# Feed-forward gate and up products of a decoder layer: from pairs of tiles with the weights stationary to four pairs of tiles with the tokens stationary

## The chip, the cores and the metric

The kernel runs on one core of one Trainium2 chip. The metric is the device time of one execution in microseconds (us). The kernel before took 1340.99 us, the median of three runs (1340.22 to 1342.37). One further execution was recorded by the hardware profiler; its own time is 1339.9 us, its span from the first to the last instruction 1338.1 us.

## What is computed

One layer of a decoder on 512 tokens of width 1024: a feed-forward half-step, a token mixing of three branches, and a second feed-forward half-step, each between two RMS norms. All is float32. The change concerns the two feed-forward steps alone:

```python
def swiglu(x, w_gu, w_down):          # x: 512 x 1024
    g, u = jnp.split(x @ w_gu, 2, axis=-1)   # w_gu: 1024 x 5632
    return (jax.nn.silu(g) * u) @ w_down     # w_down: 2816 x 1024

h = h + 0.5 * rmsnorm(swiglu(rmsnorm(h, pre_w), w_gu, w_down), post_w)
```

The width 2816 is 22 tiles of 128 columns, in the gate as in the up half of `w_gu`.

## The kernel before, in words

**Precision.** Every float32 operand of a matmul is split into a high part (ScalarE writes it, rounded: `split`, L173) and a low part (VectorE writes the rest: L168). A product is then three matmuls: high by high, high by low, low by high.

**Seven products for eight.** The gate and up columns of the same index are computed together. The token matrix is cut into quarters (256 tokens by 512 of the 1024 input columns), and so is the pair of weight tiles (512 input rows by the gate or the up tile). Winograd's form of Strassen's scheme gets the four quarters of the result from seven quarter products, numbered 1 to 7, at the price of sums and differences of quarters. The token sums t1 to t4 are made once per feed-forward step (`combine`, L244). The weight sums s1 to s4 are made for each pair (`wops`, L313): one or two of them by a DMA that accumulates (L334), the others by VectorE. The results are put together from PSUM (`pair`, L411, and `gu`, L600).

**Form of a product.** In `product` (L393) the weights are the stationary operand (128 x 128) and the tokens move, 256 columns at a time, so that the result has the gate or up columns on the partitions and the tokens along the free axis. This is the form in which the down projection needs it as its stationary operand. One pair of tiles takes 7 x 4 x 3 = 84 matmuls of 256 columns.

**Order.** The first two gate and two up tiles (the heads) are done without the scheme. The other twenty pairs follow one by one. The 22 tiles are grouped into chunks (`CHUNKS1` and `CHUNKS2`, L44), and while a chunk's pairs are computed, the down products of the chunk before it are mixed in (L680): one call of `down` is one token tile and one half of the output columns, 12 matmuls of 512 columns for a chunk of four. Their sums go to `y` in SBUF. The down products of the last chunk (six tiles in the first step, four in the second) come at the end, with the norm behind them. Except for the opening and the last two token tiles, the engine order is set by the compiler's scheduler, which follows the order of the code and the clock that the code advances by `tick`.

**Buffers.** Weight pieces arrive in `st` (4 buffers), `sum` (5) and `st2` (2); split weights lie in `w` (18), everything else in 37 slots of 128 x 512 (`s`). PSUM has 5 banks `ps` and 3 banks `px`. SyncE (SP) issues nearly all loads, in one queue and in order; GpSimd (POOL) issues the accumulating DMAs.

## Time and profile before

| | before |
|---|---|
| median of three runs | 1340.99 us |
| profiled execution, its own time | 1339.9 us |
| its span | 1338.1 us |
| TensorE (PE) busy | 1325.7 us, 99% |
| VectorE (DVE) busy | 1043.0 us, 78% |
| ScalarE (ACT) busy | 753.9 us, 56% |
| DMA, mean over the span | 137 GB/s |
| granted TensorE clock | 0.999 of full speed |

In this profile a matmul's duration reaches over the start of the next one, since matmuls are pipelined. What one matmul costs is read from the distance between two starts, not from its duration. The same holds for VectorE to a lesser degree.

### The profile page before, as it was taken

To read this page: it belongs to the slowest core of one execution; us is meant where nothing else is said; L and a number is where in the kernel's file an instruction comes from. 1 tells how busy PE (TensorE), PEld (TensorE's weight loads), DVE (VectorE), ACT (ScalarE), POOL (GpSimd) and SP (SyncE) were. 2 spreads that over 40 slices of the span, in tenths; PEclk is the share of its full clock that TensorE was granted. 3 is DMA by queue.
4 is the path that set the end of the run, shared out by engine and by line. 5 is a ranking of instruction groups with operands and counts; after the bars stand their busy time and mean duration, and the time that the engine had idled before them with its cause. 6 is when DMAs were issued, how large, how long until landed. Compare 5 with 4: busy or idle time off the path is not lost.

```text
span 1338.1 us, 24335 instructions
## 1 busy us (share of the span) xinstructions
PE 1325.7 (99%) x9228; PEld 1234.3 (92%) x9228; DVE 1043.0 (78%) x1979; ACT 753.9 (56%) x1557; POOL 87.3 (7%) x116
## 2 busy tenths in 40 slices
PE   9999999999999999999999999999999999999997
PEld 8999999999898988899899999999899999999996
DVE  7987777687897975699769968888488877777765
ACT  7764544465566764455765755566366644445541
POOL 1011110110100000000000000000011111111100
PEclk9999999999999999999999999999999999999999
DMA  9587556565425335434223423334536766556523
GB/s 252 153 191 172 144 147 165 126 160 191 161 65 157 111 98 175 122 106 125 65 79 112 119 80 95 103 106 150 193 111 161 187 162 153 143 142 154 146 64 126
DMA packets 238611, 183.14 MB, mean 137 GB/s; under 512 B 11129, under 2 KB 200990, under 8 KB 238494
## 3 DMA queue, kind: packets, MB, share of 16 engines
q1 hardware_dynamic: 223702, 159.49, 39.6%
q0 software_dynamic: 10368, 18.88, 8.6%
q10 hardware_dynamic: 4424, 3.22, 0.8%
q8 instruction: 72, 1.18, 0.4%
q14 instruction: 45, 0.37, 0.1%
HBM read 153.21 MB, written 9.47 MB: 122 GB/s over the span
## 4 chain that ended last, share of the span: by engine, by line
PE 64%; DVE 2%; DMA 1%; ACT 0%; issue 0%; POOLq 0%; DVEq 0%; ACTq 0%
PE ps L381 16%; PE ps L399 12%; PE ps L400 12%; PE ps L401 12%; PE px L381 7%; PE px L386 4%; PE px L390 1%; DVE w L168 1%; DMA st<-in_ffn_w_gu_dram 0%; DVE s L168 0%; DMA sh<-in_w_in_dram 0%; DMA st<-in_w_out_dram 0%; DVE s L736 0%; ACT w L173 0%; DVE st L996 0%
## 5 line engine op out<-in xcount | busy, mean ns | idle before, releaser
L173 ACT ACTIVATE w<-sum 128x512 fp32r<-128x512 f32 x288 | 180.3, 631 | 210.4 <-PE ps L400 183.4
L168 DVE TENSOR_TENSOR w<-sum,w 128x512 fp32r<-128x512 f32 x288 | 196.8, 687 | 72.8 <-ACT w L173 71.8
L399 PE MATMUL ps<-xhi,w 128*128 128x256 f32 x864 | 244.7, 283 | 0.1
L400 PE MATMUL ps<-xlo,w 128*128 128x256 f32 x864 | 244.5, 283 | 0.0
L401 PE MATMUL ps<-xhi,w 128*128 128x256 f32 x864 | 244.5, 283 | 0.0
L173 ACT ACTIVATE w<-st 128x512 fp32r<-128x512 f32 x240 | 150.1, 630 | 116.2 <-PE ps L400 84.0
L168 DVE TENSOR_TENSOR w<-st,w 128x512 fp32r<-128x512 f32 x248 | 168.5, 687 | 32.1 <-ACT w L173 29.4
L381 PE MATMUL px<-s,s 128*128 128x512 f32 x816 | 193.0, 390 | 0.0
L168 DVE TENSOR_TENSOR s<-s,s 128x256 f32<-128x256 f32 (+3 forms) x317 | 176.4, 562 | 14.9 <-ACT s L173 3.9
L381 PEld LDWEIGHTS px<-s,s 128*128 128x128 f32 x816 | 150.6, 188 | 29.9 <-DVE s L168 0.4
L399 PEld LDWEIGHTS ps<-xhi,w 128*128 128x128 f32 x864 | 165.5, 192 | 2.5 <-ACT s L408 0.5
L400 PEld LDWEIGHTS ps<-xlo,w 128*128 128x128 f32 x864 | 165.5, 192 | 2.0
L401 PEld LDWEIGHTS ps<-xhi,w 128*128 128x128 f32 x864 | 165.5, 192 | 0.0
L168 DVE TENSOR_TENSOR sum<-sum,st 128x512 f32<-128x512 f32 x176 | 120.3, 685 | 7.1 <-issue 3.9
L168 DVE TENSOR_TENSOR s<-s,ps 128x256 f32<-128x256 f32 (+1 forms) x195 | 93.0, 477 | 29.2 <-PE ps L381 22.1
L399 PE MATMUL ps<-t3hi,w 128*128 128x256 f32 x288 | 83.6, 290 | 0.0
L168 DVE TENSOR_TENSOR s<-s,px 128x512 f32<-128x512 f32 x73 | 49.8, 683 | 43.0 <-PE px L381 34.8
L399 PE MATMUL ps<-t4hi,w 128*128 128x256 f32 x288 | 82.1, 285 | 0.0
L399 PE MATMUL ps<-t1hi,w 128*128 128x256 f32 x288 | 82.0, 285 | 0.0
L401 PE MATMUL ps<-t2hi,w 128*128 128x256 f32 x288 | 81.7, 284 | 0.0
L401 PE MATMUL ps<-t3hi,w 128*128 128x256 f32 x288 | 81.7, 284 | 0.0
L399 PE MATMUL ps<-t2hi,w 128*128 128x256 f32 x288 | 81.6, 283 | 0.0
(198 smaller groups left out, 2996.6 us busy)
## 6 DMA issues: line engine op xcount, KB each, us to landing
st<-in_ffn_w_gu_dram SPq DMA_DIRECT2D x48, 512.0 KB, 5.0
st<-in_w_in_dram SPq DMA_DIRECT2D x48, 512.0 KB, 3.8
st<-in_ffn_w_down_dram SPq DMA_DIRECT2D x44, 512.0 KB, 4.0
sum<-in_ffn_w_gu_dram SPq DMA_DIRECT2D x80, 256.0 KB, 3.4
sh<-in_ffn_w_gu_dram SPq DMA_DIRECT2D x40, 256.0 KB, 3.3
sum<-st POOLq DMA_DIRECT2D x40, 256.0 KB, 3.3
sum<-sh POOLq DMA_DIRECT2D x32, 256.0 KB, 3.6
sum<-in_w_in_dram SPq DMA_DIRECT2D x32, 256.0 KB, 2.9
```

The lines of the kernel that those rows point to most:

```text
L168: ins = self.nc.vector.tensor_tensor(out=out, in0=a, in1=b, op=op)
L173: self.pin(self.nc.scalar.activation(hi, src, AF.Copy))
L381: self.pin_pe(mm(out, lhsT=lhs[l], rhs=rhs[r], start=a, stop=b))
L386: self.nc.tensor.matmul(out, lhsT=lhsT, rhs=rhs, start=start, stop=stop, **k)
L390: self.pin_pe(self.nc.tensor.transpose(out, in_, self.ident))
L399: mm(out, lhsT=lh, rhs=rh, start=first and k == 0, stop=False, skip_group_check=True)
L400: mm(out, lhsT=lh, rhs=rl, start=False, stop=False, skip_group_check=True)
L401: mm(out, lhsT=ll, rhs=rh, start=False, stop=k == 3, skip_group_check=True)
```

## The change

The twenty pairs of a feed-forward step become five groups of four pairs (`wide`, one per group): four gate tiles side by side are one block of 512 columns, four up tiles another.

- **Product.** In `wide_product` the tokens are stationary (128 tokens by 128 input columns) and 512 weight columns move. A product of a group is 2 token tiles x 4 x 3 = 24 matmuls of 512 columns into two banks, a group 168.
- **Weights.** Pieces are 128 rows by 512 columns. Operands 5 and 7 of a group are formed by DMA (a load and an accumulating load, both from HBM); in each step's first group operand 5 is formed by VectorE. Operands 6 and 3 are VectorE additions into the buffers of operands 1 and 2.
- **Turning the result.** The result now has tokens on the partitions. For each group and token tile the product of silu(gate) and up is transposed on VectorE in blocks of 32 x 32 (`Turn`), stored to DRAM, read back in another order (both on SP's queue), and split into high and low parts. That makes 4 block transpositions, 4 stores and 4 loads back per group, 40 of each in the kernel.
- **Down products.** A unit is now one tile and one half of the output columns for all four token tiles: 12 matmuls into four banks. `DOWNS` says how many units stand behind which product of a group. Of the last group's input in the first step one tile (`TAIL`) is left to the final part, which so has five tiles instead of six.
- **Order.** From the second group on, `strict` holds every engine to the order of the code, which is written out by hand. Background tasks are advanced only outside of these groups. One such task (loading and preparing small parameters of the token mixing) so runs at the end of the first step.

The core of the diff, without the unchanged helpers:

```diff
-CHUNKS1 = (2, 4, 4, 4, 2, 6)
-CHUNKS2 = (2, 4, 4, 4, 4, 4)
+DOWNS = ((0, 1, 0, 1, 0, 1, 1), (0, 0, 2, 2, 2, 1, 1), (0, 0, 2, 2, 1, 0, 0), (0, 0, 1, 1, 1, 0, 0), (0, 0, 1, 0, 1, 0, 0))
...
+EARLY, TAIL = 2, 1
...
+        def add(n):
+            if n == 6:
+                for k, x in enumerate(rest):
+                    self.tt(raw[5][k], raw[5][k], x, ALU.add)
+            raw[n] = raw[{6: 1, 3: 2}[n]]
+            for k in range(4):
+                self.tt(raw[n][k], raw[n][k], raw[{6: 5, 3: 6}[n]][k], ALU.add)
+
+        def cut(j):
+            return [self.wsplit(raw[j][k]) for k in range(4)]
...
+    def wide_product(self, banks, w, j, first=True):
+
+        x = self.xop[j]
+        for t in range(2):
+            ts = slice(t * P, (t + 1) * P)
+            for k in range(4):
+                lh, ll = x[0][:, k, ts], x[1][:, k, ts]
+                for n, (l, r) in enumerate(((lh, w[k][0]), (lh, w[k][1]), (ll, w[k][0]))):
+                    self.pin(self.nc.tensor.matmul(banks[t], lhsT=l, rhs=r, start=first and k == n == 0, stop=k == 3 and n == 2, skip_group_check=True))
+                self.tick(3 * 0.2268)
...
-                        gu(begun or next(pairs), act[-1])
-                        begun = None
-                if before:
-                    for i in range(8 * j // n, 8 * (j + 1) // n):
-                        down(i % NT, i // NT, before[2], ws, before[0] == 0)
...
+        class Turn:
...
+                ins = nc.vector.transpose(blocks.rearrange("p (b f i) -> p f b i", b=4, f=4), g.rearrange("p (f j b) -> p f b j", f=4, b=4))
...
+                self.pin(nc.sync.dma_start(out=d.mem.rearrange("a j b x -> (a j) (b x)"), in_=d.blocks))
...
+                ins = nc.sync.dma_start(out=d.x.rearrange("p (a x) -> p a x", a=4), in_=d.mem.rearrange("a j b x -> (j b) a x"))
...
+            self.wide_product(p, w[s, 4], 4, False)
+            d.make(d.done + 2)
+            d.evict()
+            for i in range(2):
+                self.tt(v[i], v[i], u[i], ALU.subtract)
...
+            cut(s + 1, 1)
+            q = two()
+            for i in range(2):
+                self.tt(q[i], p[i], u[i], ALU.subtract)
+                self.tt(g[i], g[i], q[i], ALU.mult)
+                turns[i] = Turn(g[i])
+                turns[i].store()
...
+                wides[s + 1][1](6)
+            d.run(plan[5])
+
+            self.wide_product(c, w[s, 3], 3, False)
+            d.make(d.done + (3 if end else 2))
+            d.run(plan[6])
+            g = two()
+            for i in range(2):
+                turns[i].back()
+            for i in range(2):
+                self.tt(g[i], u[i], c[i], ALU.add)
+                self.copy(g[i], g[i], AF.Silu)
+                self.tt(g[i], g[i], v[i], ALU.mult)
+                turns[2 + i] = Turn(g[i])
+                turns[2 + i].store()
...
+            def early_rest(turns=turns):
+                for i in range(2, 4):
+                    turns[i].back()
+
+            def late_rest(hl=hl, turns=turns):
+                for i in range(NT):
+                    hl[i] = hl[i] or turns[i].act()
+            late = early_rest, d.evict, late_rest
```

`late` is called in the next group: the loads back of the last two token tiles behind its first product, the addition of the old down sums to `y` and the splitting of the turned tiles behind its second. A group's products stand in the order 1, 2, 6, 5, 7, 4, 3.

How the instructions move is shown at three places. In each the instruction's line comes first, then its operation, what it writes and what it reads (for a matmul the moving operand first, the stationary one second).

TensorE, first feed-forward step, the end of a pair's last product and the down products behind it. Before, `t4` is the token operand of product 4, `w` a weight, `px` the bank of a down product, and `s` the weights and activations of the down product:

```order
L399 MATMUL ps391_1933<-t4hi_98,w399_1999 128x256
L400 MATMUL ps391_1933<-t4lo_99,w399_1999 128x256
L401 MATMUL ps391_1933<-t4hi_98,w400_2000 128x256
L381 MATMUL px403_2025<-s331_1666,s118_603 128x512
L381 MATMUL px403_2025<-s332_1667,s118_603 128x512
L381 MATMUL px403_2025<-s331_1666,s119_604 128x512
```

In the change, the end of a group's product 3 (`xhi1`, `xlo1` are the tokens) and the unit of down products behind it:

```order
L650 MATMUL ps464_1924<-w507_2089,xhi1_89 128x512
L650 MATMUL ps464_1924<-w508_2090,xhi1_89 128x512
L650 MATMUL ps464_1924<-w507_2089,xlo1_91 128x512
L780 MATMUL px511_2097<-s517_2153,s431_1811 128x512
L780 MATMUL px511_2097<-s518_2154,s431_1811 128x512
L780 MATMUL px511_2097<-s517_2153,s432_1812 128x512
```

The gate and up matmuls have changed places of their operands and are twice as wide; the down matmuls keep their form.

VectorE, first step. Before, the evictions of one pair's results amid weight splits (`w`) of the next:

```order
L168 TENSOR_TENSOR s443_2212<-s425_2104,ps431_2127 128x256
L168 TENSOR_TENSOR w498_2462<-st449_2252,w497_2461 128x512
L168 TENSOR_TENSOR s444_2213<-ps434_2145,s425_2104 128x256
L168 TENSOR_TENSOR s443_2212<-s443_2212,s444_2213 128x512
L168 TENSOR_TENSOR w504_2485<-sum502_2481,w503_2484 128x512
L168 TENSOR_TENSOR s416_2074<-s443_2212,s415_2073 128x512
```

In the change, the end of a group: the last block transposition (L817) of the first half of the tokens, the four additions for the next group's operand 6, the gate, product and transposition of the second half of the tokens (banks `ps463` and `ps464` are those of product 3), and the first split of the next group's operand 2:

```order
L817 STREAM_TRANSPOSE s531_2185<-s440_1828 128x4x4x32
L168 TENSOR_TENSOR st490_2003<-st490_2003,sum451_1873 128x512
L168 TENSOR_TENSOR st490_2003<-st490_2003,sum452_1876 128x512
L168 TENSOR_TENSOR st491_2005<-st491_2005,sum453_1879 128x512
L168 TENSOR_TENSOR st491_2005<-st491_2005,sum454_1882 128x512
L168 TENSOR_TENSOR s533_2241<-s401_1695,ps463_1923 128x512
L168 TENSOR_TENSOR s533_2241<-s533_2241,s494_2033 128x512
L817 STREAM_TRANSPOSE s537_2250<-s533_2241 128x4x4x32
L168 TENSOR_TENSOR s534_2242<-s402_1696,ps464_1924 128x512
L168 TENSOR_TENSOR s534_2242<-s534_2242,s495_2034 128x512
L817 STREAM_TRANSPOSE s539_2257<-s534_2242 128x4x4x32
L168 TENSOR_TENSOR w546_2290<-st509_2093,w545_2289 128x512
```

The evictions are 512 wide instead of 256, the transpositions are new, and all of the second half's chain now stands ahead of the next group's weight splits. ScalarE's silu stands between the addition and the product of each token tile.

SP's queue, first step. Before, loads of weights alone (`st`, `sum` and `sh` are buffers of gate, up and down weights):

```order
L155 DMA st553_2801<-in_ffn1_w_down_dram 128x2x512
L155 DMA st558_2811<-in_ffn1_w_down_dram 128x2x512
L155 DMA sum567_2827<-in_ffn1_w_gu_dram 128x4x128
L155 DMA sum568_2830<-in_ffn1_w_gu_dram 128x4x128
L155 DMA st565_2823<-in_ffn1_w_gu_dram 128x8x128
L155 DMA sh566_2825<-in_ffn1_w_gu_dram 128x4x128
```

In the change, at the end of a group (`turn` is the DRAM scratch):

```order
L145 DMA st509_2093<-in_ffn1_w_gu_dram 128x2x512
L145 DMA st510_2095<-in_ffn1_w_gu_dram 128x2x512
L825 DMA turn530_2181<-s529_2179 128x512
L825 DMA turn532_2187<-s531_2185 128x512
L830 DMA s535_2243<-turn530_2181 128x4x128
L830 DMA s536_2245<-turn532_2187 128x4x128
L825 DMA turn538_2252<-s537_2250 128x512
L825 DMA turn540_2259<-s539_2257 128x512
L830 DMA s553_2305<-turn538_2252 128x4x128
L830 DMA s554_2307<-turn540_2259 128x4x128
L145 DMA s555_2309<-in_ffn1_w_down_dram 128x512
L145 DMA s556_2311<-in_ffn1_w_down_dram 128x512
```

Four stores and four loads back now stand in the queue between the last gate and up load of a group and the down weights of the next, and each waits for what it moves.

More of the change, by code (lines that the diff above doesn't have):

```diff
@@ L114, in tick @@
         self.t += us
-        while not self.polling:
+        while not self.polling and self.opening == self.strict:
             due = [x for x in self.tasks if x[0] <= self.t]
@@ L288, in wsplit @@
         hi, lo = self.unit(src.shape, slot), self.unit(src.shape, slot)
-        self.split(hi, lo, src)
+        with ExitStack() as wait:
+            for ins in () if self.strict else self.opened:
+                wait.enter_context(self.tc.issue_after(ins))
+            self.split(hi, lo, src)
         return hi, lo
@@ L588, in ffn @@
+    def ffn(self, w_gu, w_down, w_post, ready, reload, after, early, last=False):
         nc = self.nc
@@ L625, in new_act, with down, cut, fetch @@
             return self.slot(dt=F32R), self.slot(dt=F32R)
-        def down_weights(f, hf):
-            st = self.load(w_down, f, 2, hf * 512, 512)
-            return [self.wsplit(st[:, j, :], slot=True) for j in range(2)]
-        def down(t, hf, act, ws, first, bank=self.paux, cs=slice(0, 512)):
-            acc = bank((P, cs.stop - cs.start))
-            self.proj_N(acc, act, slice(t * P, (t + 1) * P), [(w[0][:, cs], w[1][:, cs]) for w in ws])
-            if first:
-                nc.scalar.copy(y[t][hf], acc)
-            else:
-                self.tt(y[t][hf][:, cs], y[t][hf][:, cs], acc, ALU.add)
+        def down(t, hf, cs):
+            acc = self.psum((P, cs.stop - cs.start))
+            lhs = act(t)
+            for k in [*range(2, n), 0, 1]:
+                self.mm3(acc, lhs[k], [x[:, cs] for x in ws[k, hf]], k == 2, k == 1)
+            self.tt(y[t][hf][:, cs], y[t][hf][:, cs], acc, ALU.add)
+        tail = 0 if last else TAIL
+        wides = [self.wide(w_gu, f * P, DFF + f * P, f == early) for f in range(early, NF, 4)]
+        w = {}
+        def cut(s, j):
+            if s < len(wides):
+                w[s, j] = wides[s][2](j)
+        def fetch(s, j):
+            if s < len(wides):
+                wides[s][0](j)
         tasks, heads = [], []
@@ L686, in ffn @@
[L686 to L696 removed]
+        fetch(0, 1), fetch(0, 2), fetch(0, 5)
@@ new lines, in ffn, with begin @@
+        bank = lambda: [self.psum() for _ in range(2)]
+        two = lambda: [self.slot() for _ in range(2)]
+        def begin(s):
+            a, u = bank(), two()
+            self.wide_product(a, w[s, 1], 1)
+            return a, u
+        if resumed:
+            self.need(*tasks[0])
+            for wg, ac in heads:
+                gu_plain(wg, ac, slice(0, HT))
+            cut(0, 1)
+            begun = begin(0)
+            self.need(*tasks[1])
+        for wg, ac in heads:
+            gu_plain(wg, ac, slice(HT, T))
@@ new lines, in ffn, with final_load, final_cut @@
+        ws, spare = {}, list(self.spare())
+        rows = {}
+        def final_load(*fs):
+            for j in fs:
+                rows[j] = self.load(w_down, NF - 4 - tail + j, 1, 0, D)
+        def final_cut(*fs):
+            for j in fs:
+                for hf in range(2):
+                    if j < 2:
+                        ws[j, hf] = self.wsplit(rows[j][:, 0, HALVES[hf]])
+                    else:
+                        ws[j, hf] = spare.pop(0)
+                        self.split(*ws[j, hf], rows[j][:, 0, HALVES[hf]])
@@ L700, in ffn @@
         if last:
-            self.last_tiles(lambda t, hf, cs: down(t, hf, act, [w[hf] for w in ws], False, self.psum, cs), y, gain, h, after)
+            self.last_tiles(down, y, gain, h, after)
             return tasks
```

259 lines of the change are left out of this document (205 added, 54 removed).

## The prediction

> **What bounds the kernel now.** I read the busy times and the chain that ended last first, then who waited for whom, then the windows, then single starts.
>
> ```profile
> span 1338.1 us, 24335 instructions
> PE 1325.7 (99%) x9228; PEld 1234.3 (92%) x9228; DVE 1043.0 (78%) x1979; ACT 753.9 (56%) x1557; POOL 87.3 (7%) x116
> PE 64%; DVE 2%; DMA 1%; ACT 0%; issue 0%; POOLq 0%; DVEq 0%; ACTq 0%
> ```
>
> TensorE is busy for all but 12.4 us. Its windows (length, then busy time and instructions of PE, PEld, DVE, ACT, POOL, then clock, DMA share, GB/s) say where these lie:
>
> ```profile
> 0.00:20.00 20.00, 17.44 (x109) 15.30 (x110) 13.11 (x25) 16.16 (x37) 2.94 (x11) 1.00 0.94 280
> 40.00:60.00 20.00, 20.00 (x159) 19.54 (x159) 19.68 (x36) 14.92 (x30) 1.74 (x2) 1.00 0.71 184
> 330.00:340.00 10.00, 10.00 (x46) 8.29 (x45) 5.53 (x10) 2.47 (x8) 0.56 (x1) 1.00 1.03 364
> 1120.00:1200.00 80.00, 80.00 (x553) 74.82 (x552) 58.70 (x103) 38.66 (x75) 8.69 (x11) 1.00 0.63 159
> 1300.00:1338.10 38.10, 30.70 (x160) 26.27 (x158) 21.27 (x39) 7.73 (x21) 2.52 (x4) 0.95 0.34 118
> ```
>
> 2.6 us at the start, 7.4 us behind the last matmul; inside a feed-forward step (1120 to 1200) none. So this kernel is as long as its matmuls, and a matmul's price is the distance between starts. The rows on both sides of a change of width (start, duration, count):
>
> ```profile
> 206.20 0.28 PE L399 MATMUL ps<-t4hi,w 128*128 128x256 f32 x1
> 207.64 5.63 PE L381 MATMUL px<-s,s 128*128 128x512 f32 x24
> 213.10 0.28 PE L399 MATMUL ps<-xhi,w 128*128 128x256 f32 x1
> 1309.99 0.39 PE L381 MATMUL ps<-t2hi,s 128*128 128x512 f32 x1
> 1311.35 0.39 PE L381 MATMUL ps<-w,s 128*128 128x512 f32 x1
> ```
>
> From 206.20 to 207.64 lie the last 12 matmuls of a product, 256 wide: 0.1200 us each. From 207.64 to 213.10 lie 24 matmuls 512 wide: 0.2275. From 1309.99 to 1311.35 lie 6: 0.2267. Twice the width costs less than twice the time: about 0.013 us of each matmul does not depend on its width. A whole pair with its down products bears the prices out; in the chain two such blocks lie 15.54 us apart, and 84 x 0.1200 + 24 x 0.2275 = 15.54:
>
> ```profile
> 1101.31 5.47 PE px L381 x24
> 1116.85 5.47 PE px L381 x24
> ```
>
> **The wider matmuls.** Before: 2 steps x 20 pairs x 84 = 3360 matmuls of 256. After: 2 x 5 groups x 168 = 1680 of 512. Both 512-wide matmuls above are down products or the final ones, whose stationary operand is token data and whose moving operand is weights: the new form exactly. Each saves 2 x 0.1200 - 0.2275 = 0.0125 or - 0.2267 = 0.0133 us: 21.0 to 22.3 us, I take 21.7. The down products number 1056 on both sides and keep their width. Nothing else leaves TensorE, so this is also the most that can be gained. [...]
>
> **Does VectorE keep up?** A group in the middle takes TensorE 168 x 0.2267 + 8 units x 12 x 0.2267 = 59.9 us. Its VectorE work is 70 operations 512 wide (28 weight splits, 8 for down weights, 8 sums, 8 additions to y, 4 splits of turned tiles, 14 evictions and products) and 4 transpositions.
>
> ```profile
> L168 DVE TENSOR_TENSOR w<-sum,w 128x512 fp32r<-128x512 f32 x288 | 196.8, 687 | 72.8 <-ACT w L173 71.8
> 328.00 3.09 DVE L168 TENSOR_TENSOR w<-st,w 128x512 fp32r<-128x512 f32 x5
> 1.34 0.43 DVE L478 COPY s<-ident 128x512 f32<-128x512 f32 x1 [0.20 <-POOL ident masks.py:199]
> 336.38 0.21 DVE L192 TENSOR_SCALAR v<-ss,ss 128x1 f32<-128x1 f32 x1 [0.79 <-ACT s L186]
> L204 DVE SCALAR_TENSOR_TENSOR s<-s,r,s 128x512 f32<-128x512 f32 x20 | 14.1, 749 | 5.9 <-POOL r L195 5.8
> 1101.87 0.69 DVE L168 TENSOR_TENSOR s<-s,s 128x512 f32<-128x512 f32 x1
> 1102.60 0.63 ACT L173 ACTIVATE s<-s 128x512 fp32r<-128x512 f32 x1 [0.74 <-DVE s L168]
> 1103.26 0.69 DVE L168 TENSOR_TENSOR s<-s,s 128x512 fp32r<-128x512 f32 x1
> ```
>
> One takes 0.687, but five in a row take 3.09, so 0.60 from start to start: 70 x 0.60 = 42.0. No block transposition is in this trace. From below it is the 512-wide copy, 0.43; from above I take its 16 blocks of 32 x 32 columns as 16 operations like the smallest quoted one (0.21): 3.4 us. The nearest row is an operation of the same size, 0.69; I take that. Then VectorE has 44.8 of 59.9 us. In the old form it had 58.70 of 80, the same share: the 256-wide evictions that fall away pay for the transpositions. ScalarE has some 50 operations of 0.63, 32 us.
>
> **The seam between two groups.** Sums are not enough, since the order is fixed. With a group's first matmul at 0, its last products stand thus: 4 until 49.0, one unit, 3 from 51.7 to 57.2, one unit, end 59.9. VectorE reaches the four additions for operand 6 behind the first half's transpositions: the last split of the next operand 1 is held until product 4 gives back its `w` buffer (49.0, then ScalarE 0.63 and VectorE 0.69: 50.3), two chains of three operations follow (to 54.1), the additions end at 56.5. Then twice: addition 0.69, silu 0.63, product 0.69, transposition 0.69, with the hand-overs of the rows above (0.04 and 0.03): 62.0, which is 2.1 into the next group. Operand 2's low parts follow at 2.8, 3.4, 4.0, 4.6. TensorE, in the next group's product 2 from 5.4, asks for them at 5.7, 6.3, 7.0, 7.7. Slack 2.9 us, no wait. Four transpositions lie on this chain.
>
> The turned tiles' way through DRAM, by issue to landing:
>
> ```profile
> h<-s SPq DMA_DIRECT2D x16, 256.0 KB, 2.0
> s<-h SPq DMA_DIRECT2D x16, 256.0 KB, 5.0
> s<-v SPq DMA_DIRECT2D x12, 256.0 KB, 3.8
> ```
>
> The last store starts at 2.1, lands at 4.1; the load back at 7.9 to 9.1 (`v` is read back in pieces like these, `h` in whole rows). VectorE comes to these tiles at about 14, TensorE at 16.3. Behind the load back in SP's queue stand the next two down weights, landing at about 9; VectorE wants them at about 10.5. One microsecond of slack; a later landing delays the first unit by as much. Traffic grows from about 9 MB per four pairs to 11 MB per group (four pairs' weights by 7 MB, down 2, turning 2), 184 GB/s where 159 stand in the window from 1120 and 364 have been moved in that from 330. I cost the middle groups, eight seams in all, at nothing; the cover is the 2.9 and the 1 us.
>
> **The openings.** There VectorE is full already (19.68 of 20 us from 40 to 60), and the change wants all four splits of operand 1 amid the token sums. Before, at the three places where the new order has them or what stands before them:
>
> ```profile
> 27.66 0.68 DVE L168 TENSOR_TENSOR w<-st,w 128x512 fp32r<-128x512 f32 x1
> 37.95 0.41 DVE L168 TENSOR_TENSOR s<-s,ps 128x256 f32<-128x256 f32 x1
> 994.56 2.51 PE ps L381 x21
> 998.65 11.65 PE ps L381 x95
> 1003.77 1.02 DVE L168 TENSOR_TENSOR s<-s,s 128x512 f32<-128x512 f32 x2
> ```
>
> In the first step the first split keeps the place at 27.66, and the others follow the operation at 37.95 with sums between them: done at 39.0, 40.5 and 41.7. That operation reads the heads' last bank, so product 1 starts at about 37.4 and comes to these blocks (8, 14 and 20 matmuls on) at 39.2, 40.6 and 41.9. In product 2, where sums stand between the splits too, I find 0.5 us of waiting. In the second step the heads' first half ends at 997.1 and their second starts at 998.65. In the new order the second block of operand 1 takes the place at 1003.77 and is done at 1004.5, while TensorE, behind 8 wide and 32 narrow matmuls, is there at 1002.9: 1.5 us. At the two ends of the steps the last splits of the final down weights come 8.4 us after the last product (the seam's chain to 4.8, then six operations of 0.60) and are wanted after three units and two input tiles, 8.2 + 1.4 = 9.6: a cover of only 1.2, for which I put 0.5 us each. Openings and ends: 3 us, between 0 and 8 (each of the four by a further 1.2 us, two operations).
>
> **Sum.** 1339.9 (profiled execution; span 1338.1 and 1.8 around it) - 21.7 + 3.0 = 1321.2. The median of the runs is 1.1 higher: 1322.
>
> **The rivals.**
> *Late seams.* The eight seams cost 1 to 2 us each, because the hand-overs or the round trip are slower than I took them. For it: the landing of `s<-h` is 1.2 above that of `s<-v`, and the slack for the down weights is 1 us. Against: the 2.9 us at operand 2, and the turned tiles' 5 us. 8 x 1.5 = 12: 1334.
> *Slow transposition* (the other side). The block transposition is paced by its blocks, or by its reading in steps of four elements. All four of a group stand ahead of operand 2, so a seam loses 4 x (T - 0.69) - 2.9; the whole gain (18.7 / 8 = 2.3 per seam) is lost at T = 2.0. At 3.4 us a seam loses 7.9 us, eight 63: 1385. For it: nothing like it has been timed here. Against: the 512-wide rows quoted above lie between 0.43 and 0.75. [...]
> *No saving.* The wide matmul with three operands split is paced by something else and costs 2 x 0.1200. [...] Against: the pair's 15.54 us are made of just these prices.
>
> **Chances.** The forecast (1317 to 1327) 0.62; late seams (1327 to 1337) 0.20; slow transposition or another wait in every seam that costs over 22 us, 0.08; no saving, 0.06; below 1317, 0.04. The range 1317 to 1337 leaves out 0.18. A measurement of this kernel tells 0.2%, 2.7 us, from no change: faster 0.86, within 0.06, slower 0.08.
>
> **What would show it.** Right: PE starts in `wide_product` 0.227 apart; a group of 59.9 us; PE idle of some 15 us in all; L817 near 0.69; no PE wait for `w` at the seams. Wrong: L817 above 2 us, or PE idle of over 1 us at each product 2 or at the first unit of each group, with the load back or the down weight as releaser.

## The result and the profile after

| | before | after |
|---|---|---|
| median, executions taken in turn on one chip | 1340.61 us (1339.37 to 1342.37, 4) | 1331.17 us (1330.72 to 1333.62, 4) |
| ratio | | 0.9932, 95% interval 0.9915 to 0.9950 |
| profiled execution: span | 1338.1 us | 1328.9 us |

The change makes the kernel 9.4 us faster; 19 were forecast. A second series of five gave 1330.28 us, ratio 0.9925 (0.9912 to 0.9937). From the profile page of the changed kernel, the busy times and the transfers of the turned tiles:

```profile
PE 1308.1 (98%) x7545; PEld 1146.1 (86%) x7545; DVE 1056.6 (80%) x1919; ACT 717.5 (54%) x1456; POOL 88.8 (7%) x116
turn<-s SPq DMA_DIRECT2D x40, 256.0 KB, 2.1
s<-turn SPq DMA_DIRECT2D x40, 256.0 KB, 2.9
```

TensorE has 17.6 us less work and 20.8 us of idle time where it had 12.4. Inside the groups nothing is lost. Two links of the chain of work that ended last, in the changed kernel's second step (start, length, link):

```profile
1118.06 16.32 PE ps L650 x72
1177.90 16.32 PE ps L650 x72
```

72 wide matmuls in 16.32 us are 0.2267 us each, and the groups lie 59.84 us apart, without a wait at a seam (the passage from one group to the next).

Where the time goes is read from equal places in the two programs, in both timelines of TensorE. At the first final tile of the second step the two programs take its inputs in another order, so the rows differ there; the place is its first matmul. Before:

```profile
323.80 2.91 PE L381 MATMUL px<-s,s 128*128 128x512 f32 x12
388.04 0.28 PE L399 MATMUL ps<-t1hi,w 128*128 128x256 f32 x1
931.80 5.63 PE L381 MATMUL ps<-s,w 128*128 128x512 f32 x24
949.20 0.39 PE L381 MATMUL ps<-t2hi,s 128*128 128x512 f32 x1
1308.63 1.52 PE L381 MATMUL ps<-w,s 128*128 128x512 f32 x6
1330.42 0.28 PE L381 MATMUL ps<-t1hi,s 128*128 128x256 f32 x1
```

After (the last row holds six matmuls 0.12 apart; the last starts at 1319.31):

```profile
313.15 2.20 PE L780 MATMUL px<-s,s 128*128 128x512 f32 x9
383.95 0.28 PE L402 MATMUL ps<-t1hi,w 128*128 128x256 f32 x1
927.16 5.63 PE L384 MATMUL ps<-s,w 128*128 128x512 f32 x24
947.86 0.39 PE L384 MATMUL ps<-t2hi,s 128*128 128x512 f32 x1
1297.51 0.39 PE L384 MATMUL ps<-t2hi,s 128*128 128x512 f32 x1
1318.71 0.88 PE L384 MATMUL ps<-w,s 128*128 128x256 f32 x6
```

| place | lead of the changed kernel | since the place before | forecast |
|---|---|---|---|
| first step, behind its last product | 10.6 us | +10.6 | 10.85 - 0.5 |
| mixing, first pair of products | 4.1 | -6.5 | -0.5 |
| mixing, end | 4.6 | +0.5 | 0 |
| output projection, behind its first 48 matmuls | 1.3 | -3.3 | 0 |
| second step, first final tile | 11.1 | +9.8 | 10.85 - 1.5 |
| last matmul | 11.1 | 0 | 0 |
| end of the span | 9.2 | -1.9 | -0.5 |

So both steps gain what was forecast, and 11.7 us are lost at three places outside of the groups. At the first, the waits alone (the distances between TensorE's starts beyond what the same matmul usually takes, from 300 to 400 us) add up to 5.0 us, where there were none before. The smallest ones are left out of this sum; a matmul behind a wait, for one, starts its successor some 0.1 us late (321.70 to 322.04 in the changed kernel: 0.34 us for 0.23). With them it is 6.5, the whole loss of the place. Who is waited for, by the list of waits of the whole changed kernel (total us, times, longest; the output projection's come first):

```profile
PE ps L384 <- ACT s L173: 1.7, 2, 0.9
PE px L393 <- DVE s L204: 1.1, 3, 0.5
PE ps L384 <- DVE s L168: 0.7, 1, 0.7
...
PE ps L384 <- ACT s L838: 0.2, 1, 0.2
```

L838 and `s L168` are the turned tiles' splits at the first final tile, L204 the token tiles' norm (L393 transposes them). `ACT s L173` is the split of the mixing's result for the output projection; on ScalarE it stands behind the splits of that projection's weights. VectorE at the end of the first step, in the timeline (each row: start, length, operation, in brackets the idle time before it and its releaser):

```profile
321.16 0.69 DVE L168 TENSOR_TENSOR s<-s,s 128x512 f32<-128x512 f32 x1 [0.70 <-ACT s L589]
321.89 1.12 DVE L817 STREAM_TRANSPOSE s<-s 128x512 f32<-128x512 f32 x1
322.93 1.25 DVE L168 TENSOR_TENSOR s<-s,s 128x512 fp32r<-128x512 f32 x2
324.09 2.49 DVE L168 TENSOR_TENSOR w<-st,w 128x512 fp32r<-128x512 f32 x4
...
338.34 0.69 DVE L168 TENSOR_TENSOR s<-s,s 128x512 f32<-128x512 f32 x1 [0.84 <-DMA s<-in_ffn_post_w_dram]
```

The transposition takes 1.09 us, not 0.69. The splits that the first final tile needs come at 322.93; TensorE was there at 321.3. The last splits of the final down weights follow from 324.09 to 326.58, 13.4 us behind the last product's end (313.15). The post-norm gain (`post_w`) is late as well; SP's queue says why:

```profile
323.46 2.07 SPq L830 DMA_DIRECT2D s<-turn  x2
325.58 1.01 SPq L155 DMA_DIRECT2D st<-in_w_in_dram  x2
326.69 5.89 SPq L145 DMA_DIRECT2D s<-in_x_dram  x8
332.94 1.00 SPq L145 DMA_DIRECT2D s<-in_ffn_post_w_dram  x2
```

It is issued behind the turned tiles' loads back, which wait for their stores, and behind eight loads of the residual.

In the output projection TensorE waits 0.9 and 0.8 us, and behind that it runs at half clock. Its rows after, the row of the same 27 matmuls before, and two windows after (length, busy times, then clock, DMA share, GB/s), over the stretch and behind it:

```profile
937.76 1.23 PE L384 MATMUL ps<-w,s 128*128 128x512 f32 x3 [0.89 <-ACT s L173]
939.82 8.20 PE L384 MATMUL ps<-w,s 128*128 128x512 f32 x27 [0.83 <-ACT s L173]
```

```profile
942.69 6.67 PE L381 MATMUL ps<-w,s 128*128 128x512 f32 x27 [0.49 <-ACT s L173]
```

```profile
940.00:943.50 3.50, 3.47 (x8) 2.26 (x9) 2.04 (x4) 0.69 (x2) 0.00 (x0) 0.51 0.59 145
943.50:945.00 1.50, 1.50 (x8) 1.23 (x8) 0.00 (x0) 0.00 (x0) 0.00 (x0) 1.00 0.83 267
```

Before, they took 6.67 us behind one wait of 0.49. At the end, the last 29 us of the changed kernel: 19.6 us of TensorE, then 9.3 without it, where there were 7.4.

```profile
1300.00:1328.90 28.90, 19.59 (x98) 16.53 (x96) 19.96 (x38) 6.61 (x19) 2.83 (x4) 0.89 0.46 165
```

### The profile page after: what moved, and what is told of

Its sections match the earlier page's. It is cut to its first block, busy times and chain, and to the rows that moved or that the text cites. A ratio compares the mean times of both kernels' runs of the same rounds, so it can differ in the third digit from the quotient of the medians.

```text
span 1328.9 us, 20915 instructions
## 1 busy us (share of the span) xinstructions
PE 1308.1 (98%) x7545; PEld 1146.1 (86%) x7545; DVE 1056.6 (80%) x1919; ACT 717.5 (54%) x1456; POOL 88.8 (7%) x116
## 4 chain that ended last, share of the span: by engine, by line
PE 83%; DVE 9%; DMA 2%; ACT 2%; issue 1%; POOL 1%; SPq 0%; POOLq 0%; DVEq 0%; ACTq 0%
PE ps L650 28%; PE ps L384 14%; PE px L780 10%; PE ps L402 7%; PE ps L404 7%; PE ps L403 7%; PE px L389 4%; PE ps L780 3%; DVE s L168 3%; DVE w L168 1%; PE px L393 1%; POOL r L195 1%; ACT s L186 1%; DVE s L204 1%; DVE xlo L168 1%
## 5 line engine op out<-in xcount | busy, mean ns | idle before, releaser
L168 DVE TENSOR_TENSOR w<-st,w 128x512 fp32r<-128x512 f32 x368 | 240.2, 684 | 58.9 <-ACT w L173 56.1
L168 DVE TENSOR_TENSOR s<-s,s 128x512 f32<-128x512 f32 (+3 forms) x347 | 213.1, 633 | 78.7 <-ACT s L589 50.5
L173 ACT ACTIVATE w<-st 128x512 fp32r<-128x512 f32 x360 | 212.5, 626 | 76.4 <-PE ps L403 31.0
L650 PE MATMUL ps<-w,xhi 128*128 128x512 f32 x480 | 148.9, 391 | 1.5 <-DVE w L168 0.8
L173 ACT ACTIVATE w<-sum 128x512 fp32r<-128x512 f32 x178 | 108.4, 633 | 62.4 <-PE ps L403 46.5
L168 DVE TENSOR_TENSOR w<-sum,w 128x512 fp32r<-128x512 f32 x178 | 119.1, 684 | 19.8 <-ACT w L173 19.4
L589 ACT ACTIVATE s<-ps 128x512 f32<-128x512 f32 x84 | 48.8, 594 | 134.7 <-PE ps L650 134.6
L168 DVE TENSOR_TENSOR s<-s,ps 128x512 f32<-128x512 f32 (+1 forms) x171 | 96.6, 569 | 22.7 <-PE ps L384 17.4
L402 PE MATMUL ps<-xhi,w 128*128 128x256 f32 x384 | 108.8, 283 | 0.0
L404 PE MATMUL ps<-xhi,w 128*128 128x256 f32 x384 | 108.7, 283 | 0.0
L403 PE MATMUL ps<-xlo,w 128*128 128x256 f32 x384 | 108.7, 283 | 0.0
L650 PEld LDWEIGHTS ps<-w,xhi 128*128 128x128 f32 x480 | 89.7, 188 | 21.7 <-DVE w L168 1.8
L650 PE MATMUL ps<-w,xlo 128*128 128x512 f32 x240 | 93.2, 389 | 0.0
L384 PE MATMUL ps<-w,xhi 128*128 128x512 f32 x256 | 80.6, 394 | 0.1
L173 ACT ACTIVATE s<-s 128x512 fp32r<-128x512 f32 (+1 forms) x98 | 58.5, 609 | 40.4 <-DMA s<-in_ffn_w_down_dram 30.7
L384 PE MATMUL ps<-s,w 128*128 128x512 f32 (+1 forms) x384 | 80.2, 364 | 0.0
L402 PEld LDWEIGHTS ps<-xhi,w 128*128 128x128 f32 x384 | 73.6, 192 | 0.7 <-ACT s L411 0.2
L403 PEld LDWEIGHTS ps<-xlo,w 128*128 128x128 f32 x384 | 73.6, 192 | 0.5
```

What stands on the lines that cost most here:

```text
L168: ins = self.nc.vector.tensor_tensor(out=out, in0=a, in1=b, op=op)
L173: self.pin(self.nc.scalar.activation(hi, src, AF.Copy))
L384: self.pin_pe(mm(out, lhsT=lhs[l], rhs=rhs[r], start=a, stop=b))
L402: mm(out, lhsT=lh, rhs=rh, start=first and k == 0, stop=False, skip_group_check=True)
L403: mm(out, lhsT=lh, rhs=rl, start=False, stop=False, skip_group_check=True)
L404: mm(out, lhsT=ll, rhs=rh, start=False, stop=k == 3, skip_group_check=True)
```

## The experiments

All diffs are against the changed kernel. W is the sum of TensorE's waits from 300 to 400 us, O that of the 65 us around the output projection, E the time from the start of the last matmul to the end, H the stretches of 3.4 us at half clock that the trace shows up to the last matmul; the ratios are against the kernel before, in turn on one chip. The series ran on several chips, so rows are compared by their ratios, and where two intervals overlap a difference is not shown. In `e4_turn_twice` everything comes later, so that the 100 us of W reach less far into the mixing.

| run | median us | ratio (95%) | W | O | E | H |
|---|---|---|---|---|---|---|
| before | 1340.61 | | -0.3 | 0.5 | 7.7 | 0 |
| after | 1331.17 | 0.9932 (0.9915 to 0.9950) | 5.0 | 2.2 | 9.6 | 1 |
| `r_after` | 1330.28 | 0.9925 (0.9912 to 0.9937) | 5.2 | 1.7 | 9.6 | 0 |
| `e1_out_first` | 1329.28 | 0.9918 (0.9904 to 0.9933) | 4.7 | 1.3 | 9.8 | 0 |
| `e2_ends` | 1336.00 | 0.9966 (0.9953 to 0.9979) | 5.2 | 1.7 | 11.9 | 2 |
| `e3_tail2` | 1334.19 | 0.9958 (0.9943 to 0.9972) | 8.4 | 1.7 | 9.7 | 2 |
| `e4_turn_twice` | 1369.38 | 1.0217 (1.0200 to 1.0234) | 7.6 | 1.9 | 9.6 | 8 |
| `e5_adds_first` | 1331.30 | 0.9923 (0.9907 to 0.9938) | 3.7 | 2.5 | 10.0 | 2 |
| `e6_read_rows` | 1329.39 | 0.9907 (0.9890 to 0.9923) | 4.9 | 2.1 | 9.6 | 1 |
| `e7_four_loads` | 1334.57 | 0.9949 (0.9929 to 0.9969) | 4.5 | 1.6 | 11.5 | 2 |
| `e8_prep` | 1329.01 | 0.9908 (0.9893 to 0.9922) | 4.8 | 2.2 | 9.6 | 0 |
| `e9_gain_early` | 1330.72 | 0.9924 (0.9911 to 0.9938) | 4.5 | 2.7 | 8.5 | 0 |
| `e9b_gain_only` | 1327.84 | 0.9906 (0.9891 to 0.9921) | 3.9 | 1.7 | 7.8 | 0 |
| `e10_all` | 1328.80 | 0.9914 (0.9900 to 0.9927) | 4.4 | 1.3 | 8.4 | 0 |
| `f1_lat10` | 1329.90 | 0.9922 (0.9907 to 0.9936) | 3.5 | 2.4 | 7.8 | 2 |
| `f2_pool_gain` | 1332.80 | 0.9947 (0.9924 to 0.9969) | 6.5 | 1.6 | 7.8 | 1 |
| `f3_three` | 1326.17 | 0.9896 (0.9881 to 0.9910) | 3.8 | 1.2 | 8.2 | 0 |
| `f4_three_lat` | 1326.09 | 0.9898 (0.9883 to 0.9913) | 3.4 | 0.9 | 8.2 | 0 |

**The changed kernel again.**

> The changed kernel once more, unaltered, beside the runs that follow. If its losses sit in the program (theory): again about 1331, waits of 4.5 to 5.5 us between 300 and 392 us, two waits of about 1 us in the output projection, 9.6 us behind the last matmul. What differs from its first trace is what varies from one execution to the next: by the runs so far the waits below 12 us (1 to 3 us) and the stretch at half clock.

W and E are the program's. The stretch at half clock is not in this trace (clock 1.00 from 930 to 945 us): the same program has it in some executions. By the mean clock (0.996 or less in six of the nine, 0.997 or 0.998 in three), most have one.

**The output projection's loads first.**

```diff
                 w[1].append((hi, lo))
+        self.anchor = self.brought     # the last load issued so far
         h = reload()
```

> All eight loads of the output projection's weights stand ahead of every feed-forward load of the second step in SP's queue (in the changed kernel eleven loads of 256 KB for its first group stand among them). If these loads make the projection wait for its weights (theory), its two gaps of 0.9 and 0.8 us and the stretch at half clock behind them go: 1331.2 - 1.3 - 1.5 = about 1328. If the projection waits for its weights for another reason (rival: ScalarE and VectorE come late to the splits), the gaps stay and the time is 1331. If the held loads are then missing at the second step's opening, the gaps there (0.6 and 0.8 us) grow by more than 1 us and the time is 1331 or above.

Transfers that SP issued around the projection's beginning, from 895 to 932 us, changed kernel (KB each, median us from issue to landing, of those whose landing is on the trace):

```profile
st<-in_w_out_dram SPq DMA_DIRECT2D x8, 512.0 KB, 5.2
sh<-in_ffn_w_gu_dram SPq DMA_DIRECT2D x6, 256.0 KB, 3.1
sum<-in_ffn_w_gu_dram SPq DMA_DIRECT2D x5, 256.0 KB, 3.7
```

In the kernel before, from 899 to 936 us:

```profile
st<-in_w_out_dram SPq DMA_DIRECT2D x8, 512.0 KB, 3.7
sum<-in_ffn_w_gu_dram SPq DMA_DIRECT2D x4, 256.0 KB, 3.0
sh<-in_ffn_w_gu_dram SPq DMA_DIRECT2D x2, 256.0 KB, 3.1
```

Eleven loads of 256 KB stand among the projection's in SP's queue instead of six (GpSimd issues three more), and the last of the projection's eight is late. It is issued 1.1 us ahead of the projection's first matmul in the changed kernel (931.49 and 932.63), 4.0 us ahead in the kernel before (933.25 and 937.27), and 2.5 us ahead in this run (930.01 and 932.52). ScalarE's split of it, in the kernel before, the changed kernel and this run:

```profile
938.40 0.63 ACT L173 ACTIVATE t4hi<-st 128x512 fp32r<-128x512 f32 x1 [0.52 <-DMA st<-in_w_out_dram]
```

```profile
936.56 0.63 ACT L173 ACTIVATE t4hi<-st 128x512 fp32r<-128x512 f32 x1 [0.90 <-DMA st<-in_w_out_dram]
```

```profile
935.17 0.63 ACT L174 ACTIVATE t4hi<-st 128x512 fp32r<-128x512 f32 x1 [1.24 <-DMA st<-in_w_out_dram]
```

That is 1.1, 3.9 and 2.7 us behind the projection's first matmul. So the other loads cause a part of the lateness; what is left with them out of the way is not explained (in all three, SP last waits for a buffer that VectorE gives back). O falls to 1.3 (0.5 in the kernel before), and the mean clock is 0.998 in all four executions; the opening behind it does not suffer. The gain, 1 to 2 us, is less than the 3 expected, and the interval overlaps that of the changed kernel, whose second trace has an O of 1.7. O is as low in `e10_all` (1.3) and in `f3_three` (1.2), which have the same edit.

**Order at the steps' ends.** In `e2_ends` the turned tiles' splits stand behind each silu, and the last additions to `y` ahead of the last tiles' splits:

```diff
                 self.copy(g[i], g[i], AF.Silu)
+                if end:
+                    hl[i] = turns[i].act()
                 self.tt(g[i], g[i], v[i], ALU.mult)
...
-                late[0](), late[2](), late[1]()
+                late[0](), late[1](), late[2]()
```

> At the end of each step the splits of the first two turned tiles move between the silu waits of the last half (they stood behind both transpositions), and the last additions to y move ahead of the splits of the last two turned tiles. Same operations, another order. If VectorE's lateness at a step's end is what the first step's end and the mixing's first 60 us lose (theory), the waits of 0.4 and 0.9 us at the first final tile go, VectorE comes some 2 us earlier to the post-norm, at least half of the 3.7 us of waits between 343 and 382 us go, and the end behind the last matmul shrinks from 9.3 towards 7.4 us: 1331.2 - 1.3 - 2 - 1.5 = about 1326. If the waits in the mixing come from the final part being shorter (five row blocks instead of six, rival), only the first 1.3 and the end change: 1328.5.

Slower. VectorE keeps the order of the code, and a split behind a silu waits for ScalarE twice: 1.2 us for each half instead of 0.7. The first final tile is no longer waited for, but everything behind is later, and at the end the gain lands 2.3 us after VectorE wants it (E 11.9). The idea was right about the first tile and wrong about what is next. In `e5_adds_first` both additions come first, then both products and transpositions:

```diff
             for i in range(2):
                 self.tt(g[i], u[i], c[i], ALU.add)
                 self.copy(g[i], g[i], AF.Silu)
+            for i in range(2):
                 self.tt(g[i], g[i], v[i], ALU.mult)
                 turns[2 + i] = Turn(g[i])
                 turns[2 + i].store()
+                if end:
+                    hl[i] = turns[i].act()
```

> In the last half of every group both additions are issued ahead of both silus' products, so that VectorE does not stand idle for 0.70 us behind each silu (the second run of experiments lost 1.2 us there instead of 0.7, since it put a split behind each silu); at a step's end the splits of the first two turned tiles follow one behind each transposition. Same operations. Theory (VectorE's place in the order at the steps' ends is what is lost): VectorE is 1.4 us earlier behind the last transposition, the wait of 1.3 us at the first final tile goes, the waits between 343 and 382 us shrink from 3.7 by about 1.4, and the end behind the last matmul from 9.6 by about 1: 1331.2 - 1.3 - 1.4 - 1 = 1327.5. Rival (the turned tiles' round trip or the order of loads sets these waits): the first final tile is no longer waited for, nothing else moves: 1330.

The 0.70 us behind each silu are gone, and the wait at the first final tile with them. The next wait takes its place: 2.4 us at the first token tile's transposition (344.4, for L204), because on VectorE that tile now waits for the gain. VectorE's timeline of this run:

```profile
338.09 0.69 DVE L168 TENSOR_TENSOR s<-s,s 128x512 f32<-128x512 f32 x1 [2.01 <-DMA s<-in_ffn_post_w_dram]
```

That is nearer to the rival, which named the order of loads: the late load of the gain stood hidden behind VectorE's lateness.

**A longer final part.**

```diff
-EARLY, TAIL = 2, 1
+EARLY, TAIL = 2, 2
```

> The first step's final part has six row blocks as in the kernel before (one more than in the changed kernel), so two units (5.4 us of matmuls) move from ahead of it into it. If the shorter final part is why the mixing's first tiles are late (rival), the 3.7 us of waits between 343 and 382 us mostly go: about 1328. If VectorE's lateness at the last products is the cause (theory), the first final tile is now asked for 2.7 us sooner and waits longer, and the sum of the waits from 310 to 390 us stays within 1 us of the 5.0 in the changed kernel: 1330 to 1333.

The rival falls, but the theory's sum of 5 us is missed too: TensorE waits 4.8 us (for L838) at the first final tile, since two units less stand ahead of it, and the waits behind that are still 3.5 us, though the final part is 5.4 us longer.

**The transposition: its price and its slack.** Twice, into the same place:

```diff
                 self.pin(ins)
+                ins = nc.vector.transpose(...)    # the same once more
+                self.pin(ins)
```

> Each of the 40 block transpositions is done twice, into the same place: 1.0 us more of VectorE each. By the trace of the changed kernel operand 2 is ready about 1.8 us before TensorE asks for it at each seam, and the four transpositions of a group stand on the chain to it: four more cost 4.0 - 1.8 = 2.2 us at each of eight seams, and up to 2 us at each of the two ends: 1331 + 18 + 4 = about 1353. If the chain of the seam is not what the forecast took it for (rival: some of the extra time falls into the waits of 0.7 us for silu, or TensorE waits elsewhere), a seam loses less than 1 us: below 1340.

TensorE in the third group's product 2:

```profile
155.94 0.50 PE L650 MATMUL ps<-w,xhi 128*128 128x512 f32 x1 [2.94 <-ACT s L589]
156.94 0.50 PE L650 MATMUL ps<-w,xhi 128*128 128x512 f32 x1 [0.50 <-DVE w L168]
```

Six of the eight seams lose 2.6 to 3.8 us each, at product 2, where the chain of the seam said 4.0 - 1.8 = 2.2; that is some 17.6 in all; the seams into the second group of each step lose 0.7 and nothing. L589 is ScalarE's eviction, which stands behind the late silu: the chain's last link is another one than the forecast named. With the ends (4.4 and 2.3 us, where the changed kernel has 1.3 and none) that is 23 us more of waits, close to the 22 expected. Of the other 15 us of the 38, 12 are the clock: seven stretches more, 1.7 us each. A window behind the seam shown (clock third from the end):

```profile
158.00:162.00 4.00, 4.00 (x12) 3.16 (x11) 4.00 (x8) 0.45 (x1) 0.00 (x0) 0.57 0.78 229
```

Why 1.09 us? The transposition reads every fourth column. Adjacent columns instead:

```diff
-... g.rearrange("p (f j b) -> p f b j", f=4, b=4)
+... g.rearrange("p (f b j) -> p f b j", f=4, b=4)
```

> The transposition reads 32 adjacent columns into each block instead of every fourth column; the features of a turned tile then stand in another order than the rows of the down weights, so this kernel computes another function with the same work. Theory (reading in steps of four elements is what made the transposition 1.09 instead of 0.69 us): L817 takes 0.65 to 0.75 us, VectorE has 16 us less work, the chain at each step's end is 1.6 us shorter, and 1.3 us at the first final tile and about 1 us each in the mixing and at the end come back: 1331.2 - 3 = 1328. Rival (the blocks set the pace): L817 stays at 1.09 us, and the time at 1331.

All transpositions of this run, and of the changed kernel (ns: shortest, median, longest):

```profile
L817 DVE STREAM_TRANSPOSE s<-s x40: 699/711/715, 78.6 to 1294.0; 128x512 f32<-128x512 f32 x40
```

```profile
L817 DVE STREAM_TRANSPOSE s<-s x40: 1075/1088/1124, 77.0 to 1294.5; 128x512 f32<-128x512 f32 x40
```

0.71 against 1.09: the reading in steps cost 0.38 us, not the blocks. In time it is worth some 1 to 2 us, and the intervals overlap: the first final tile is not waited for any more, and the first token tile waits 1.8 us instead, for the gain (2.0 us on VectorE, as in `e5_adds_first`). Putting the features' order right with four loads back,

```diff
-                ins = nc.sync.dma_start(out=d.x..., in_=d.mem.rearrange("a j b x -> (j b) a x"))
+                for b in range(4):
+                    ins = nc.sync.dma_start(out=d.x[32 * b:32 * b + 32, :]..., in_=d.mem[:, :, b, :].rearrange("a j x -> j a x"))
```

> As the run before, with the order of the features put right on the way back: four loads of 64 KB for each turned tile instead of one of 256 KB, 120 more DMA issues on SP's queue at 0.37 us. If the shorter transposition is worth something and SP's queue has room (theory): within 1 us of the run before, about 1328 to 1329. If the issues or the smaller loads are late (rival): the load back lands 1.1 us later, its slack at the seams being about 1 us by the forecast; then waits at the first unit of each group appear, 8 x 1, and the time is 1333 to 1340.

loses more than the shorter transposition brings, but not at the seams, which stay without waits: at the ends, where the gain and the residual stand behind these issues (E 11.5, 2.8 us of wait at 357).

**The parameters' task.**

```diff
     def prepare():
-        yield 100.0
+        yield 45.0
```

> The small task that prepares the gate's parameters (four small loads, one transposition on TensorE, some nine VectorE operations of 0.2 us, one exponential on ScalarE) runs in the first group, as it did in the kernel before near 100 us, instead of at the end of the first step. If its work there is part of why the mixing's first tiles come late (theory): 1 to 2 us of the 3.7 between 343 and 382 us go, 1329.5. If VectorE's backlog from the last group alone makes them late (rival): under 0.5 us change, 1331.

W hardly moves (4.8) and E not at all. The median is 1.3 to 2.2 us lower, but the intervals overlap, and none of its executions has a clock below 0.997; whether the task's own work or the missing stretch is what it gains isn't told apart.

**The gain.**

```diff
             g = two()
+            if end:
+                gain = self.bcast_gain(w_post)
             for i in range(2):
                 turns[i].back()
...
         h = reload()
-        gain = self.bcast_gain(w_post)
```

> The early loads of the gain alone, with the order of the last half as it was. Theory: only the 0.8 us that VectorE waited for the gain at the first step's end goes there, the 1.3 us at the first final tile stay, and the end behind the last matmul shrinks to about 8: about 1328.5. If the order of VectorE alone mattered at the end (rival): 9.6 us behind the last matmul, 1330.5.

Two loads are issued earlier, and E is back at 7.8 (7.7 in the kernel before): the whole loss at the end was the gain's. In the last 29 us of the changed kernel VectorE multiplied by the gain only after 1309; here it does so in a gap at 1305.56, so that it isn't behind when the last tile comes:

```profile
1305.56 1.89 DVE L168 TENSOR_TENSOR s<-s,s 128x512 f32<-128x512 f32 x3
```

W falls by 1.1. With the additions first:

> The additions first, as in the run of that name, and the two loads of the post-norm gain (256 KB each) issued ahead of the turned tiles' loads back in the last group, not behind them and the eight loads of the residual. Theory (SP's queue, held by the turned tiles' last loads back, brings the gain late, and that now sets the first token tile): the wait of 2.0 us for the gain on VectorE goes, the wait of TensorE at the first tile's transposition falls from 2.5 to below 1 us, the waits from 300 to 400 us from 3.7 to about 2, the end behind the last matmul from 9.6 to 10 us to about 8: 1331 - 1.3 - 1.7 - 1.7 = about 1326.5. Rival (VectorE's own backlog sets it): the first tile comes no earlier, sum of waits 3.5 or more, 1330.

The wait for the gain is gone here too, but W stays at 4.5, as the rival had it, and the run comes out slower than the gain alone (1330.72 against 1327.84 in the same series, though the intervals overlap a little): new waits stand at the final weights (0.75 us at 324) and in the output projection.

> Four edits together: the additions first, the gain early, the output projection's loads first, the parameters' task in the first group. If the losses that these take away are separate (theory): 1331.2 - 3.0 - 1.7 - 2.0 - 1.0 = about 1323.5, no stretch at half clock, and a sum of waits from 300 to 400 us below 2. If they cover one another, or a new wait takes their place (rival): 1327 to 1330.

This is the rival: the four edits together are no better than the three without the additions first (`f3_three` below, 0.9896, intervals again overlapping a little).

**What is left at the first step's end.** Two runs were to tell a chain that is too long for its place from a VectorE that is full.

```diff
-... norm=8.0, ...
+... norm=10.0, ...
```

> As the run with the gain alone, and the planner's guess of the time from a tile's post-norm to its transposition is 10 us instead of 8, so that TensorE's order has these transpositions (of both steps) some 2 us of its work later. If the waits of 0.3 to 0.9 us at each token tile between 343 and 372 us are only transpositions that stand too early in TensorE's order (theory A): they go, the sum from 300 to 400 us falls from 3.9 to about 2.3, 1326. If VectorE is full there and everything behind waits for it (theory B): the sum stays within 0.7 of 3.9, the waits stand further behind (370 to 390), 1328.

```diff
-            self.tt(y[t][0], y[t][0], gain[0], ALU.mult)
+            nc.gpsimd.tensor_tensor(out=y[t][0], in0=y[t][0], in1=gain[0], op=ALU.mult)
```

> As the run with the gain alone, and the first step's eight products of y with the post-norm gain (0.69 us each on VectorE, 5.5 us in all) are done by GpSimd. If VectorE's load between 320 and 390 us is what TensorE waits for (theory B): the waits from 300 to 400 us fall from 3.9 to below 2, 1326. If the chains' own latency is (theory A): no change, or longer by what GpSimd is slower than VectorE, 0.5 to 1 us at each tile: 1328 to 1331.

Later transpositions change W by 0.4 (3.5): theory A falls. GpSimd makes it worse (6.5), but it needs 1.5 and 1.6 us (means of its two groups of four) for what VectorE does in 0.69, and that lies on the token tiles' chain, so it is no test of a full VectorE. For that speak only the windows from 300 to 400 us, which do not hold quite the same work: VectorE 84.55 busy before, 90.75 after. Before:

```profile
300.00:400.00 100.00, 100.00 (x618) 90.01 (x617) 84.55 (x150) 59.32 (x126) 6.24 (x10) 1.00 0.43 142
```

After:

```profile
300.00:400.00 100.00, 96.83 (x520) 81.14 (x519) 90.75 (x164) 57.69 (x122) 6.82 (x11) 1.00 0.50 161
```

3.4 to 3.9 us of waits remain in the best runs. 1.3 of them are those at the first final tile, which the late chain on VectorE explains; the cause of the other 2 to 2.6 stays open. That moving the last tiles' splits or the final weights' splits off VectorE would lower them wasn't tried.

**A faster version.** The gain early, the projection's loads first and the task in the first group:

> Three edits that each made the changed kernel faster alone, together: the gain early (-2.4), the output projection's loads first (-1.9), the parameters' task in the first group (-1.5), all against the changed kernel's 1330.7. If they add up: 1325. If the stretch at half clock was a part of each (it can go only once): 1327.

> The three edits and the 10 us for the transpositions. By theory A 1.5 us below the run with the three edits, by theory B the same within 1.

The three edits give 1326.17 us, 0.9896 of the kernel before (0.9881 to 0.9910), below both intervals of the changed kernel; they do not quite add up (1325 was the sum). The later transpositions add nothing.

## Why the prediction was half right

**The wide matmuls: right.** 0.2267 us from start to start, and each step gains 10 us by the leads. The 0.013 us that the forecast read from the trace of the kernel before bore out: 2 x 0.1200 - 0.2267 = 0.0133 us for each wide matmul.

**The seams: right, with less slack than thought.** No wait at any seam, groups of 59.84 us for 59.9. One seam of the changed kernel in the timeline, TensorE's first wide matmuls of the next group and VectorE's last transposition ahead of operand 2's low parts:

```profile
207.08 0.61 PE L650 MATMUL ps<-w,xhi 128*128 128x512 f32 x2
```

```profile
209.24 1.11 DVE L817 STREAM_TRANSPOSE s<-s 128x512 f32<-128x512 f32 x1
210.27 2.45 DVE L168 TENSOR_TENSOR w<-st,w 128x512 fp32r<-128x512 f32 x4
```

The transposition ends 3.3 us into the group (forecast 2.1), the first low part at 3.9 (2.8), and it is asked for at 5.7: 1.8 us of slack for 2.9. The round trip takes 2.1 + 2.9 us, less than the 2.0 + 3.8 to 5.0 of the forecast. Late seams and no saving are out.

**The transposition: mis-sized.** 1.09 us for 0.69. It stayed below the 2.0 at which the gain would be lost, and doubling it showed that the rival was real: 38 us. "Its reading in steps of four elements" stood in the rival; it was the cause, at 0.38 us (1.09, and 0.71 in `e6_read_rows` with adjacent columns); the blocks were not. Why such reading takes longer, no run shows.

**The openings: right in size.** 0.8 us of waits for 0.5 in the first step, 1.6 for 1.5 in the second. The places are not those of the forecast: half of the first stands in product 1, and the second is three waits (0.2, 0.6 and 0.8 us), not one.

**The term that failed: "Openings and ends: 3 us", of which 0.5 for each end.** The first step's end lost 6.5 us (5.0 in waits), the second's 1.9. The cover of 1.2 us rested on "8.4 us after the last product (the seam's chain to 4.8, then six operations of 0.60)". Measured, it is 13.4 us at the first step's end and 9.9 at the second's, where TensorE does not come to wait for it. The chain itself ends 9.9 us behind product 3 at the first end (323.01 and 313.15), 6.3 at the second and 6.0 at the seam shown above. Of the 5 us above the forecast's 4.8, the transpositions at 1.09 are 1.6. The rest is the order, since the forecast took the seam's chain over to the ends. At a seam a unit of down products between products 4 and 3 gives VectorE 2.7 us; in a step's last group none stands there (`DOWNS`). And in the first step VectorE begins the chain 1.2 us behind product 4's end, in the second 1.3 us ahead of it, and has four splits of final down weights inside it, two more than in the second. So the first final tile was 1.3 late, and behind it the token tiles; how much of their waits comes from this chain stays open. What stands behind the turned tiles' loads back in SP's queue was looked at for the seams (two down weights), but not for the ends, where it is the residual and the gain. That is the 1.9 at the end, and about 1 us at the first step.

**What wasn't in the sum: the output projection, 3.3 us.** The order of SP's queue in front of the second step changed, from six loads of 256 KB among the projection's weights to eleven. The prediction follows this queue at the seams alone. About a third of the loss is longer waits (1.2 us), and about half is a stretch at half clock (1.7 us), for which no term stood either.

The range held the time, but by luck: its upper part belonged to "late seams", which isn't what happened. TensorE's idle time was forecast as 15 us and is 20.8.

## What to carry to other kernels

A gain inside a loop is handed back at its ends: cost the hand-over to the stage before and behind with the same care as the seam, and follow each in-order queue through it, DMA issues first. A wait that is removed there uncovers the next; ask what was hidden behind it before reordering, since two edits that were to remove waits (`e2_ends`, `e3_tail2`) made the kernel slower. Two loads moved ahead of a blocked one took the loss at the end away; neither reordering of VectorE made the kernel faster.

## What the runs showed of the hardware

- **Half clock stood behind short waits, in steps of 3.413 us.** In the changed kernel the granted clock is 0.5 for 3.41 us from 940.06, behind waits of 0.89 and 0.83 us, and again from 1322.35, behind the last matmul. The two starts lie 382.29 us apart, 112 times 3.413. Cut into windows by these steps, TensorE is idle for 1.72 us in the window ahead of 940.06 and for 2.76 in that ahead of 1322.35; in every other window between the first and the last matmul it is idle for 1.31 us at most, and the clock behind it is 1.00. By the clock a stretch costs half its length, 1.7 us; the 27 matmuls over that at 940.06 took 8.20 us for 6.67 before. In `e4_turn_twice`, read from windows of 2 us, the first stretch begins at 158.1, and the others up to the last matmul a whole number of steps later (the last at 1332.3: 344); one is two steps long. There 2.3 us without a matmul between 1270 and 1274 have half clock behind them, from 1274.3, while 2.3 us between 218 and 222, and again between 1142 and 1148, have none; a step begins inside each of these two, at 219.6 and at 1144.6. So in that trace the length of the idle time alone did not tell whether a stretch followed; at these three places it went with the position on the steps. The changed kernel has a stretch in one of its two traces, and an H of 1 or 2 says little about an edit. In `e4_turn_twice` the mean clock fell to 0.988 from 0.996, some 11 us of the 38.
- **The order of reading set the price of the block transposition**: 0.71 us for 128 x 512 elements with adjacent columns (`e6_read_rows`), 1.09 with every fourth (the changed kernel).
- **GpSimd took 1.5 to 1.6 us** in `f2_pool_gain` for a product of two 128 x 512 tiles that takes VectorE 0.69 in the changed kernel.
